# fp32r products that read their moving columns in turn from two halves, in a one-core decoder layer

## The chip, the cores and the metric

The kernel runs on one core of one Trainium2 chip. The metric is the device time of the program in microseconds (us), from its first to its last instruction as the device counts it.

## The reference

One decoder layer over a prompt of 1024 tokens and 8 sample tokens that share the weights, all in float32, with 1024 channels:

```python
h = rmsnorm(x, g_mix);  u = h @ w_in
a, val, gate = u[..., :512], u[..., 512:1024], u[..., 1024:]
glu = val * jax.nn.sigmoid(gate)
ya = pool_mixer(a)                      # trailing means over 2/4/8/16 tokens, a 128x128 map per group
yb = conv_mixer(glu)                    # causal depthwise conv of width 31, LayerNorm, swish
x = x + jnp.concatenate([ya, yb], -1) @ w_out
x = x + cross_attn(rmsnorm(x, g_attn), mk, mv, w_q, w_o)     # 4 heads of 256, 256 memory tokens
h = rmsnorm(x, g_ffn)
x = x + (jax.nn.silu(h @ w_gate) * (h @ w_up)) @ w_down      # 2816 hidden channels
y = rmsnorm(x, g_final)
```

The sample tokens attend to caches of their own (256 tokens each), and the last inputs of the mean pooling and of the convolution are returned as states, as are the memory keys and values.

## The kernel before

Channels lie on the 128 partitions and tokens along the free dimension: T = 1032 columns, first the 512 even prompt tokens, then the 512 odd ones, then the 8 samples. A product takes a 128 x 128 weight tile as the stationary operand and columns of tokens as the moving one, and adds up in PSUM over the channel tiles.

Every operand of a large product is kept as two fp32r parts, a rounded one and the remainder (`split`), and each product is made in three passes, `PASSES = ((0, 0), (0, 1), (1, 0))`: rounded by rounded, rounded weight by remainder, remainder of the weight by rounded. All these products are fp32r. The rest (row sums against `ones_d`, transposes, the pooling map `pmap`) are plain fp32 products.

The widths of the moving operand are few:

- 344 columns (`CW` = T / 3), three spans in three PSUM banks, in `step3` (L497): the projections w_in, w_out, w_q and w_o;
- 512 columns, or 260 columns in two banks (520 in all), in `product` (L1355): the feed-forward part, which forms seven block products for a 2 x 2 block product. A block of 512 tokens takes one bank, a block of 520 (512 tokens and the samples) takes two;
- 256 columns for the keys (L876) and the scores (L1052); 512 for the values (L953) and for probabilities by values (L1110);
- 512 or 260 columns in the last down projection (L1698).

PSUM is read by VectorE (DVE) and ScalarE (ACT). The readers that the change touches are: `gate_out` and `value_out` (from L733), `mixer_in` (L862), `keys` (L880), `values` (L958), `out_a` and `out_b` (L976, L992), `q_group` (L1030, L1031, L1033), the exponentials of the scores (L1069), `pv` (L1114, L1115), `proj_o` (L1221), `plus_sums` (L1371) and `copy_sums` (L1375) with their caller `from_sums`, and `last_down` (L1706). Helpers that lay a view over an operand are `halves` (two halves), `ch3` (three spans) and `as_banks` (the view that matches one or two banks).

The order of the work on each engine comes from a planner in the kernel (`Program.order`), which goes by costs and priorities of the tasks. Those costs depend on widths alone.

The phases on TensorE are, in order: the input projections, keys and values (about 20 to 200 us of the span), the output projection (to about 297), queries, scores and probabilities by values (to 449), w_o (to 540), the gated feed-forward part (about 560 to 980), the down projection (to 1138) and its last part (to 1209).

Of the kernel before, what the change touches and what calls it, by code (L numbers as in the profile page):

```python
# [19 lines left out]
NS = 8  # L20
# [241 lines left out]
def hybrid_step_kernel(ctx: ExitStack, tc: tile.TileContext, io):  # L262
# [34 lines left out]

    def ch3(ap):
        return ap.rearrange("p (c n) -> p c n", c=NCH)

# [190 lines left out]
    def step3(ps, w, wkeys, cols, x, k, first, last, spans=range(NCH), keys=None):  # L491


        def emit(e):
            for p, (wi, xi) in enumerate(PASSES):
                for c in spans:
                    e.matmul(ps[:, c, :CW], w[:, wi, cols], x[:, xi, c * CW : (c + 1) * CW],  # L497
                             start=first and p == 0, stop=last and p == 2)
# [234 lines left out]
    def gate_out(j, ps):  # L733
        t = scr(f"t{j}")
        tk = (t,)
        if j == 0:
            add({"ACT": act(T, True)}, lambda e: e.activation(ch3(t[:]), ps[:, :, :CW], AF.Copy), all3(ps), [tk])
            add({"DVE": dve(T), "Pool": pool_tt(T)}, lambda e: e.tensor_tensor(t[:], t[:], Rx[:], ALU.mult), RX + [tk], [tk], lock=True)
        else:
            add({"DVE": dve(T)}, lambda e: e.tensor_tensor(ch3(t[:]), ps[:, :, :CW], ch3(Rx[:]), ALU.mult), all3(ps) + RX, [tk])  # L740
# [4 lines left out]
    def value_out(j, ps, t):  # L745
# [4 lines left out]
        if j == 0:  # L750
            add({"DVE": dve(T), "ACT": act(T, True)}, lambda e: (
                e.activation(ch3(gb[:, i]), ps[:, :, :CW], AF.Copy) if e is nc.scalar else
                e.tensor_copy(ch3(gb[:, i]), ps[:, :, :CW])), all3(ps), [gk])
            add({"DVE": dve(T), "Pool": pool_tt(T)}, lambda e: e.tensor_tensor(gb[:, i], gb[:, i], t[:], ALU.mult), [gk, (t,)], [gk], lock=True)
        else:
            add({"DVE": dve(T)}, lambda e: e.tensor_tensor(ch3(gb[:, i]), ps[:, :, :CW], ch3(t[:]), ALU.mult), all3(ps) + [(t,)], [gk])
# [102 lines left out]
    def mixer_in(g):  # L859
        ps = group("w_in", xop)  # L860
        ab, ai = a2[g // 2], g % 2
        add({"DVE": dve(T)}, lambda e: e.tensor_tensor(ch3(ab[:, ai]), ps[:, :, :CW], ch3(Rx[:]), ALU.mult), all3(ps) + RX, [(ab, ai)])  # L862
# [6 lines left out]
    def keys(q):  # L869
        ps = mm_buf(f"kps{q}", 1)  # L870
        for i in range(2):
            w, wkeys = w_take("w_k")
            for k in range(KT):
                def emit(e, k=k, i=i, w=w):
                    for p, (wi, xi) in enumerate(PASSES):
                        e.matmul(ps[:, 0, i * NMEM : (i + 1) * NMEM], w[:, wi, block_cols(k)], memg[k // 4][:, xi, k % 4],  # L876
# [4 lines left out]
            kf[:], ps[:, 0].rearrange("p (i m) -> p i m", i=2), Rm().unsqueeze(1).to_broadcast([P, 2, NMEM]), ALU.mult),  # L881
# [62 lines left out]
    def values(c):  # L944
        ps = mm_buf(f"vps{c}", 2)
        for kk in range(4):
            w, wkeys = w_take("w_v")
            for k in (2 * kk, 2 * kk + 1):
                def emit(e, k=k, w=w):
                    col = (k % 2) * 512  # L950
                    for p, (wi, xi) in enumerate(PASSES):
                        for m in range(2):
                            e.matmul(ps[:, m], memg[k // 4][:, xi, k % 4, m * P : (m + 1) * P], w[:, wi, col : col + 512],  # L953
# [3 lines left out]
        for m in range(2):  # L957
            add({"ACT": act(512, True, 1)}, lambda e, m=m: e.activation(  # L958
                vf[:, m], ps[:, m], AF.Copy, scale=rmc[:, 2 * m : 2 * m + 1]), [(ps,), ("rmc",)], [(vf, m)])
# [7 lines left out]
    def out_a(n):  # L967
# [8 lines left out]
        add({"DVE": dve(T)}, lambda e: e.tensor_tensor(ch3(x1[j][:, i]), ps[:, :, :CW], ch3(x1[j][:, i]), ALU.add),  # L976
# [6 lines left out]
    def out_b(n):  # L983
# [8 lines left out]
        add({"DVE": dve(T)}, lambda e: e.tensor_tensor(ch3(x1[j][:, i]), ps[:, :, :CW], ch3(x1[j][:, i]), ALU.add), all3(ps) + [xk], [xk])  # L992
# [35 lines left out]
    def q_group(n):  # L1028
        ps = group("w_q", xq)
        add({"ACT": act(T, True)}, lambda e: e.activation(ch3(qop[n][:, 0]), ps[:, :, :CW], AF.Copy), all3(ps), [(qop[n], 0)])  # L1030
        add({"DVE": dve(T)}, lambda e: e.tensor_tensor(ch3(qop[n][:, 1]), ps[:, :, :CW], ch3(f32(qop[n][:, 0])), ALU.subtract),  # L1031
            all3(ps) + [(qop[n], 0)], [(qop[n], 1)])
        add({"DVE": 0.07}, lambda e: e.tensor_copy(qs[:, n], ps[:, 2, CW - NS : CW]), all3(ps), [("qs", n)])  # L1033

    def scores(n):
# [11 lines left out]
        def emit(e):  # L1047
            for i in range(2):
                tt = 2 * i2 + i
                for dt in range(2):  # L1050
                    for p, (ki, qi) in enumerate(PASSES):
                        e.matmul(bank()[:, i * NMEM : (i + 1) * NMEM], qop[2 * h + dt][:, qi, tt * P : (tt + 1) * P],  # L1052
                                 kk[:, ki, 2 * (h % 2) + dt], start=(dt == 0 and p == 0), stop=(dt == 1 and p == 2))
# [12 lines left out]
        def exps(e):  # L1066
            for i in range(2):
                tt = 2 * i2 + i
                e.activation(pr[:, tt], bank()[:, i * NMEM : (i + 1) * NMEM], AF.Exp, bias=st[:, 2 + i : 3 + i],  # L1069
# [29 lines left out]
    def pv(n):  # L1099
# [4 lines left out]
        for c in range(2):  # L1104
            sl = slice(c * 512, (c + 1) * 512)

            def emit(e, c=c, sl=sl):
                for m in range(2):
                    for p, (vi, pi) in enumerate(PASSES):
                        e.matmul(ps[:, c], v[:, vi, m, col : col + P], pT[h][m][:, pi, sl],  # L1110
# [3 lines left out]
            add({"ACT": act(512, True)}, lambda e, c=c, sl=sl: e.activation(oo[:, 0, sl], ps[:, c], AF.Copy), [(ps, c)], [(oo, 0, c)])  # L1114
# [764 lines left out]
```

## Time and profile before

| | us |
|---|---|
| median of 3 runs | 1219.57 |
| lowest and highest | 1217.78, 1220.19 |
| span of the profiled execution | 1217.6 |
| VectorE busy in the profiled execution | 931.2 |
| ScalarE busy | 524.8 |
| GpSimd busy | 250.1 |

A row of a group has: line, engine, operation, tiles (output, then inputs), shape, count; then busy us of all, mean ns of one; then the idle time of the engine just before them and what ended it. PE is TensorE's products, PEld its weight loads, which run beside the products. Products are pipelined, and the end of each is modelled, so that two neighbours overlap in the rows: what a stream of products costs is read from their starts, or from differences between shapes.

### The profile page before, as it was taken

To read this page: it belongs to the slowest core of one execution; us is meant where nothing else is said; L and a number is where in the kernel's file an instruction comes from. 1 tells how busy PE (TensorE), PEld (TensorE's weight loads), DVE (VectorE), ACT (ScalarE), POOL (GpSimd) and SP (SyncE) were. 2 spreads that over 40 slices of the span, in tenths; PEclk is the share of its full clock that TensorE was granted. 3 is DMA by queue.
4 is the path that set the end of the run, shared out by engine and by line. 5 is a ranking of instruction groups with operands and counts; after the bars stand their busy time and mean duration, and the time that the engine had idled before them with its cause. 6 is when DMAs were issued, how large, how long until landed. Compare 5 with 4: busy or idle time off the path is not lost.

```text
span 1217.6 us, 19433 instructions
## 1 busy us (share of the span) xinstructions
PE 1202.0 (99%) x7736; PEld 1125.9 (92%) x7736; DVE 931.2 (76%) x1548; ACT 524.8 (43%) x718; POOL 250.1 (21%) x297
## 2 busy tenths in 40 slices
PE   9999999999999999999999999999999999999997
PEld 9999988999999979999999999999999999999886
DVE  7899999766258886679877787777867798879754
ACT  7765656455135633454222322233222355544533
POOL 3568842231110102131000000000000024332101
PEclk9999999999999999999999999999999999999998
DMA  7334676326386774421332233222313597678612
GB/s 289 82 77 111 145 213 214 125 105 205 112 263 202 238 272 156 122 87 62 122 113 80 96 114 108 109 80 97 123 70 105 207 310 210 180 185 224 149 51 89
DMA packets 60170, 179.69 MB, mean 148 GB/s; under 512 B 7792, under 2 KB 11568, under 8 KB 58800
## 3 DMA queue, kind: packets, MB, share of 16 engines
q1 hardware_dynamic: 53392, 157.56, 37.1%
q0 software_dynamic: 6256, 20.54, 9.7%
q8 instruction: 60, 0.98, 0.3%
q10 hardware_dynamic: 432, 0.36, 0.1%
q14 instruction: 30, 0.25, 0.1%
HBM read 144.66 MB, written 33.78 MB: 147 GB/s over the span
## 4 chain that ended last, share of the span: by engine, by line
PE 78%; DVE 4%; DMA 1%; issue 1%; ACT 0%; POOL 0%; DVEq 0%; SPq 0%; POOLq 0%; ACTq 0%
PE pr L1355 47%; PE po L497 7%; PE fd L1698 6%; PE ps L497 5%; PE oa L497 4%; PE ob L497 4%; PE sc L1052 1%; DVE spcache_k L1149 1%; PE vps L953 1%; PE pv L1110 1%; DMA sbcache_v<-pd 1%; PE kps L876 0%; PE pmap L896 0%; DMA spcache_k<-in_cache_k 0%; DMA pd<-prow 0%
## 5 line engine op out<-in xcount | busy, mean ns | idle before, releaser
L1355 PEld LDWEIGHTS pr<-ab,wTb 128*128 128x128 f32 x1056 | 131.8, 188 | 3.5
L1355 PE MATMUL pr<-ab,wTa 128*128 128x260 f32 x1056 | 133.6, 282 | 0.2 <-DVE su L1371 0.2
L1355 PE MATMUL pr<-ab,wTb 128*128 128x260 f32 x1056 | 133.0, 282 | 0.0
L1355 PEld LDWEIGHTS pr<-ab,wTa 128*128 128x128 f32 x1056 | 130.8, 188 | 2.4 <-DVE su L1371 0.4
L1355 PE MATMUL pr<-ab,wG 128*128 128x512 f32 x528 | 129.2, 393 | 0.0
L1371 DVE TENSOR_TENSOR su<-pr,su 128x520 f32<-128x520 f32 (+1 forms) x112 | 77.7, 695 | 57.6 <-PE pr L1355 57.4
L1355 PEld LDWEIGHTS pr<-ab,wG 128*128 128x128 f32 x528 | 96.3, 188 | 19.7 <-DVE wG L396 0.4
L497 PE MATMUL ps<-xop,w 128*128 128x344 f32 x720 | 114.1, 320 | 0.0
L497 PEld LDWEIGHTS ps<-xop,w 128*128 128x128 f32 x720 | 113.6, 188 | 0.0
L1355 PEld LDWEIGHTS pr<-hb,dV 128*128 128x128 f32 x768 | 98.8, 188 | 4.1
L1355 PE MATMUL pr<-hb,dV 128*128 128x260 f32 x768 | 100.1, 283 | 0.0
L497 PE MATMUL ps<-xq,w 128*128 128x344 f32 x576 | 94.9, 322 | 0.1
L497 PEld LDWEIGHTS po<-oo,w 128*128 128x128 f32 x576 | 90.8, 188 | 0.6 <-DVE oo L1115 0.4
L497 PE MATMUL po<-oo,w 128*128 128x344 f32 x576 | 91.3, 320 | 0.0
L497 PEld LDWEIGHTS ps<-xq,w 128*128 128x128 f32 x576 | 90.8, 188 | 0.4 <-DMA w<-in_w_q 0.4
L710 DVE SCALAR_TENSOR_TENSOR cacc<-glu,vec,cacc 128x511 f32<-128x511 f32 (+14 forms) x116 | 76.9, 740 | 0.0
L1355 PE MATMUL pr<-hb,dW 128*128 128x512 f32 x288 | 74.5, 394 | 0.1
L385 ACT ACTIVATE w<-raw 128x1024 fp32r<-128x1024 f32 (+1 forms) x37 | 35.0, 950 | 86.7 <-PE po L497 24.4
L1698 PE MATMUL fd<-ho,w 128*128 128x260 f32 (+1 forms) x432 | 69.1, 321 | 0.0
L1698 PEld LDWEIGHTS fd<-ho,w 128*128 128x128 f32 x432 | 62.0, 188 | 6.9 <-issue 0.5
L1382 POOL MEMSET su<- 128x16 f32 x22 | 2.5, 113 | 318.9 <-PE pr L1355 267.7
L1355 PE MATMUL pr<-ab,wU 128*128 128x512 f32 x264 | 64.6, 393 | 0.0
(311 smaller groups left out, 2195.7 us busy)
## 6 DMA issues: line engine op xcount, KB each, us to landing
gr<-in_w_gu SPq DMA_DIRECT2D x44, 512.0 KB, 3.4
hb<-su SPq DMA_DIRECT2D x8, 1040.0 KB, 4.6
hs<-hb SPq DMA_DIRECT2D x16, 520.0 KB, 5.3
dr<-in_w_dn SPq DMA_DIRECT2D x16, 512.0 KB, 4.4
spcache_k<-in_cache_k SPq DMA_DIRECT2D x12, 512.0 KB, 5.7
hs<-hb SPq DMA_DIRECT2D x12, 512.0 KB, 4.6
raw<-in_w_in SPq DMA_DIRECT2D x10, 512.0 KB, 3.3
hb<-he SPq DMA_DIRECT2D x8, 520.0 KB, 2.8
```

Of the source, the lines that this page charges most:

```text
L385: e.activation(dst(0), src(), AF.Copy, scale=1.0 if gain is None else gain)
L497: e.matmul(ps[:, c, :CW], w[:, wi, cols], x[:, xi, c * CW : (c + 1) * CW], start=first and p == 0, stop=last and p == 2)
L710: e.scalar_tensor_tensor(acc[h][:, n:], src[:, : HALF - n], w, acc[h][:, n:], ALU.mult, ALU.add)
L953: e.matmul(ps[:, m], memg[k // 4][:, xi, k % 4, m * P : (m + 1) * P], w[:, wi, col : col + 512], start=(k == 0 and p == 0), stop=(k == KT ...
L1052: e.matmul(bank()[:, i * NMEM : (i + 1) * NMEM], qop[2 * h + dt][:, qi, tt * P : (tt + 1) * P], kk[:, ki, 2 * (h % 2) + dt], start=(dt == ...
L1110: e.matmul(ps[:, c], v[:, vi, m, col : col + P], pT[h][m][:, pi, sl], start=(m == 0 and p == 0), stop=(m == 1 and p == 2))
L1149: e.scalar_tensor_tensor(piece[:, b], piece[:, b], 1.0, bc[:, b], ALU.mult, ALU.mult, accum_out=out(m)[:, first + b : first + b + 1])
L1355: e.matmul(bank(c), w[:, wi, cols(j)], xs[0](j, xi)[:, c * n : (c + 1) * n], start=onto is None and j == 0 and p == 0, stop=j == nj - 1 an ...
L1371: from_sums(sums, "DVE", dve, lambda e, src, sl: e.tensor_tensor(as_banks(o(sl), src), src, as_banks(a(sl), src), op), [akey], [okey])
L1382: add({"Pool": 0.12}, lambda e: e.memset(o(), 0.0), [], keys)
L1698: e.matmul(view(i), w[:, wi, col : col + P], hops[k][:, xi, half, lo - half * HALF + i * width // count : lo - half * HALF + (i + 1) * wid ...
```

## The change

Each fp32r product reads its moving columns in another order. `turns` lays over n columns the view "column 0 of the first half, column 0 of the second half, column 1 of the first half, ...". The output, through `placed`, is written in PSUM in the order in which it comes, so that two neighbouring PSUM columns belong to the two halves. Every reader of such a PSUM tile takes it through `drawn`: the even columns first (the first half), then the odd ones (the second half), against two running halves of its other operands. So the values in SBUF stay where they were. Weights, transposes, row sums and the pooling map are untouched. The instructions, their number and their order on each engine are the same; the planner's costs are too.

```diff
+    def turns(ap):
+        return ap.rearrange("p (h n) -> p n h", h=2)
+
+    def placed(ap):
+        return ap.rearrange("p (n h) -> p n h", h=2)
+
+    def drawn(ap):
+        return ap.rearrange("p (n h) -> p h n" if len(ap.shape) == 2 else "p c (n h) -> p c h n", h=2)
+
+    def drawn3(ps):
+        return drawn(ps[:, :, :CW])
...
+    def ch3h(ap):
+        return ap.rearrange("p (c h n) -> p c h n", c=NCH, h=2)
...
-                    e.matmul(ps[:, c, :CW], w[:, wi, cols], x[:, xi, c * CW : (c + 1) * CW],
+                    e.matmul(placed(ps[:, c, :CW]), w[:, wi, cols], turns(x[:, xi, c * CW : (c + 1) * CW]),
                              start=first and p == 0, stop=last and p == 2)
...
-        add({"ACT": act(T, True)}, lambda e: e.activation(ch3(qop[n][:, 0]), ps[:, :, :CW], AF.Copy), all3(ps), [(qop[n], 0)])
-        add({"DVE": dve(T)}, lambda e: e.tensor_tensor(ch3(qop[n][:, 1]), ps[:, :, :CW], ch3(f32(qop[n][:, 0])), ALU.subtract),
+        add({"ACT": act(T, True)}, lambda e: e.activation(ch3h(qop[n][:, 0]), drawn3(ps), AF.Copy), all3(ps), [(qop[n], 0)])
+        add({"DVE": dve(T)}, lambda e: e.tensor_tensor(ch3h(qop[n][:, 1]), drawn3(ps), ch3h(f32(qop[n][:, 0])), ALU.subtract),
...
     def as_banks(ap, src):

-        return ap if len(src.shape) == 2 else ap.rearrange("p (c n) -> p c n", c=2)
+        return halves(ap) if len(src.shape) == 3 else ap.rearrange("p (c h n) -> p c h n", c=2, h=2)
...
-                        e.matmul(bank(c), w[:, wi, cols(j)], xs[0](j, xi)[:, c * n : (c + 1) * n],
+                        e.matmul(placed(bank(c)), w[:, wi, cols(j)], turns(xs[0](j, xi)[:, c * n : (c + 1) * n]),
                                  start=onto is None and j == 0 and p == 0, stop=j == nj - 1 and p == 2,
                                  skip_group_check=onto is not None)
...
-            add({engine: cost(sl.stop - sl.start)}, lambda e, src=src, sl=sl: emit(e, src(), sl), [key] + r, w)
+            add({engine: cost(sl.stop - sl.start)}, lambda e, src=src, sl=sl: emit(e, drawn(src()), sl), [key] + r, w)
```

The products of the keys, the values, the scores, probabilities by values and the last down projection change in the same way as in `product`, and the readers named above in the same way as in `q_group`.

More of the change, by code (lines that the diff above doesn't have):

```diff
@@ L1051, in emit @@
                     for p, (ki, qi) in enumerate(PASSES):
[L1052 to L1053 removed]
+                        e.matmul(placed(bank()[:, i * NMEM : (i + 1) * NMEM]), qop[2 * h + dt][:, qi, tt * P : (tt + 1) * P],
+                                 turns(kk[:, ki, 2 * (h % 2) + dt]), start=(dt == 0 and p == 0), stop=(dt == 1 and p == 2))
         o = 2 * (h % 2)
@@ L1697, in emit @@
                     for i in range(count):
-                        e.matmul(view(i), w[:, wi, col : col + P], hops[k][:, xi, half, lo - half * HALF + i * width // count : lo - half * HALF + (i + 1) * width // count],
+                        e.matmul(placed(view(i)), w[:, wi, col : col + P],
+                                 turns(hops[k][:, xi, half, lo - half * HALF + i * width // count : lo - half * HALF + (i + 1) * width // count]),
                                  start=(k == 0 and p == 0), stop=(k == 5 and p == 2))
```

39 lines of the change are left out of this document (20 added, 19 removed).

## The prediction

> **What bounds the kernel now.** I read the page first, then the stages, then the single groups of TensorE's work by shape, then the order of time inside one loop. The page says which engine is full:
>
> ```profile
> span 1217.6 us, 19433 instructions
> PE 1202.0 (99%) x7736; PEld 1125.9 (92%) x7736; DVE 931.2 (76%) x1548; ACT 524.8 (43%) x718; POOL 250.1 (21%) x297
> PE 78%; DVE 4%; DMA 1%; issue 1%; ACT 0%; POOL 0%; DVEq 0%; SPq 0%; POOLq 0%; ACTq 0%
> ```
>
> TensorE is busy 99% of the span and carries 78% of the chain that ended last. So the length of one product, times their number, is the time. The table by stage (us, then busy time and count of each engine, the granted clock, DMA share) shows where that holds and which engine stands second:
>
> ```profile
> 20.00:176.00 156.00, 156.00 (x995) 152.63 (x994) 148.84 (x224) 98.03 (x128) 104.98 (x83) 1.00 0.51 129
> 176.00:297.00 121.00, 120.39 (x718) 112.77 (x717) 93.16 (x105) 65.12 (x69) 29.96 (x14) 1.00 0.47 157
> 297.00:449.00 152.00, 148.89 (x963) 140.94 (x961) 99.51 (x339) 62.34 (x126) 16.64 (x24) 1.00 0.65 209
> 449.00:540.00 91.00, 91.00 (x576) 90.79 (x576) 59.85 (x128) 36.00 (x45) 16.35 (x19) 1.00 0.42 143
> 540.00:560.00 20.00, 19.82 (x107) 15.96 (x106) 18.70 (x28) 13.72 (x21) 9.65 (x10) 1.00 0.24 80
> 560.00:1032.00 472.00, 472.00 (x3165) 435.52 (x3165) 368.97 (x514) 151.05 (x195) 24.37 (x55) 1.00 0.37 126
> 1032.00:1138.00 106.00, 105.85 (x703) 97.30 (x702) 90.05 (x131) 49.06 (x57) 32.10 (x38) 1.00 0.74 194
> 1138.00:1209.00 71.00, 70.41 (x441) 62.84 (x440) 35.42 (x60) 34.68 (x58) 8.58 (x11) 1.00 0.32 87
> sum 1197.60, PE 1184.51 PEld 1108.74 DVE 918.32 ACT 510.48 POOL 242.63; mean PE 131.61 PEld 123.19 DVE 102.04 ACT 56.72 POOL 26.96
> ```
>
> The granted clock is 1.00 in every stage, so no throttle stands behind what follows. VectorE is second everywhere, with 149 of 156 us in the first stage and 369 of 472 us in the long one.
>
> Now the length of one product. A busy time that adds modelled ends is no measure of it, so I take differences between shapes. Groups by shape (count, busy us, mean ns of one):
>
> ```profile
> L1355 PE MATMUL pr<-ab,wTa 128*128 128x260 f32 x1056 | 133.6, 282 | 0.2 <-DVE su L1371 0.2
> L1355 PE MATMUL pr<-ab,wG 128*128 128x512 f32 x528 | 129.2, 393 | 0.0
> L532 PE MATMUL Rf_ps<-xss,ones_d 128*128 128x512 f32 x4 | 1.9, 592 | 0.0
> L1729 PE MATMUL fin_ps<-fin,ones_d 128*128 128x260 f32 x4 | 1.2, 382 | 0.0
> ```
>
> The first two are fp32r products, the last two plain fp32 passes, which the change leaves alone. 252 more columns cost an fp32r product 393 − 282 = 111 ns, 0.4405 ns per column. They cost a plain pass 592 − 382 = 210 ns, 0.8333 ns per column. Half of the plain figure is 0.4167. So fp32r takes columns nearly twice as fast as a plain pass, but not quite: 0.0238 ns per column are lost. The starts in one loop of the long stage (start us, busy us) say the same without modelled ends:
>
> ```profile
> 701.37 2.93 PE L1355 MATMUL pr<-ab,wG 128*128 128x512 f32 x12
> 704.14 3.04 PE L1355 MATMUL pr<-ab,wTb 128*128 128x260 f32 x24
> 707.01 3.03 PE L1355 MATMUL pr<-ab,wTa 128*128 128x260 f32 x24
> ```
>
> (704.14 − 701.37) / 12 = 230.8 ns for 512 columns, (707.01 − 704.14) / 24 = 119.6 ns for 260, a slope of 0.441. The Trainium skill, page "TensorE: Matmul & The Clock Gate", section "Back-to-back issue gap", gives about 216 ns for an isolated 512-column product; this trace has 230.8, so here something is in the way.
>
> **The change, part by part.** No instruction is added, dropped or moved on any engine, and no DMA changes. Three things differ. First, 512, 344, 260 or 256 moving columns of a product are read as column 0 of the first half, column 0 of the second half, column 1 of the first, and so on. Second, PSUM is still written in running order, so that side is as before and I cost it at nothing; if that were wrong it would show in the same start-to-start times as the first part. Third, VectorE and ScalarE read every second PSUM column, first the even, then the odd ones, and write running halves.
>
> The reading of moving columns. It can go both ways, and no row shows a moving operand with a step. The loss of 0.0238 ns per column does not come with plain passes, which take a column every 0.8333 ns. Read in turn, each half is asked for a column only every second time, which is that very pace. If the loss comes from asking the same place too fast, the change removes it. If the reader lives on neighbouring columns being fetched together, the change takes that from it, and the nearest row is again the plain pass: a column every 0.8333 ns. So the bounds are 0.4167 and 0.8333 ns per column, from 0.4405 now.
>
> I take the lower bound. The loss is small and steady: the next two rows' starts repeat the 119.6 ns with another weight tile, while VectorE comes and goes.
>
> ```profile
> 709.88 2.94 PE L1355 MATMUL pr<-ab,wG 128*128 128x512 f32 x12
> ```
>
> (709.88 − 707.01) / 24 = 119.6 ns again. A loss as steady as that belongs to the stream itself, not to other engines, and the stream's order is what changes. That is a choice, not a proof: hence the chances below.
>
> What that is worth: 0.0238 × 512 = 12.2 of 230.8 ns, 5.3%; 0.0238 × 260 = 6.2 of 119.6 ns, 5.2%. At 5.25% of PE's busy time the stages could give 8.2, 6.3, 7.8, 4.8, 1.0, 24.8, 5.6 and 3.7 us, together 62. What I let through, stage by stage:
>
> - 20 to 176: VectorE is busy 148.84 of 156, so at most 7 of 8.2 us; I take 5.
> - 176 to 297: some plain passes and LayerNorm waits lie in it; 5 of 6.3.
> - 297 to 449: the chain leaves TensorE for transfers and VectorE here; 4 of 7.8.
>
> ```profile
> 346.55 4.46 DMA pd<-prow
> 351.08 6.49 DMA sbcache_v<-pd
> 360.53 5.54 DVE spcache_k L1149 x32
> 449.07 91.27 PE po L497 x576
> 559.74 472.90 PE pr L1355 x3168
> ```
>
> - 449 to 540: one unbroken run of TensorE in the chain (91.27 us); all 4.8.
> - 540 to 560: a chain through the row factors; 0.
> - 560 to 1032: again one run of 472.90 us; VectorE has 103 us to spare; 24 of 24.8.
> - 1032 to 1138: VectorE at 90 of 106 us, DMA share 0.74; 4 of 5.6.
> - 1138 to 1209: 2.5 of 3.7. Head and tail: 0.
>
> The sum is 49.3 us.
>
> The readers. VectorE reads PSUM as fast as SBUF today:
>
> ```profile
> L1371 DVE TENSOR_TENSOR su<-pr,su 128x520 f32<-128x520 f32 x90 | 62.5, 696 | 41.5 <-PE pr L1355 41.4
> L1379 DVE TENSOR_TENSOR su<-su,Rf 128x520 f32<-128x520 f32 x44 | 30.6, 696 | 5.1 <-ACT su L1407 4.7
> L1375 ACT ACTIVATE su<-pr 128x512 f32<-128x512 f32 x24 | 14.2, 592 | 12.6 <-PE pr L1355 12.0
> ```
>
> 696 ns with an operand in PSUM, 696 ns without: PSUM is not what holds it. With a step of two I take 696 again. A gain is excluded, since the time is already that of an SBUF read, which sets the lower end; as the upper end I take twice, 1392 ns. The cover is VectorE's wait for TensorE, 41.5 us in this one group. ScalarE's readers have more room still (43% busy).
>
> The profiled execution has a span of 1217.6 us against a median of 1219.57 of the runs. 1217.6 − 49.3 = 1168.3 for the span; 1219.57 − 49.3 = 1170.3 for the time.
>
> **The rivals.**
>
> Nothing changes. The reader takes columns at 0.4405 ns whatever their order. For it: two different weight tiles gave 119.6 ns each, as a fixed rate would. Against it: plain passes show no such loss against their own round figure. Time 1219.6, chance 0.13.
>
> The readers become the bound. In the long stage the readers at L1371 are this much:
>
> ```profile
> 560.00:1032.00 472.00, 110.82 (x160) 1.00 0.37 126
> ```
>
> If each takes twice as long, VectorE has 369 + 110.8 = 480 us to do in a stage of 472, and it cannot be full: it now idles 103 us, mostly for TensorE. With half of that left the stage is 531 us. So +8 to +59 us there, and in the first stage, where VectorE is at 95%, some 8 more: 1235 to 1290, I take 1265. It decides from a lengthening of about half (369 + 55 + 51 = 475). For it: no row shows this step. Against it: the equal 696 ns. Chance 0.11.
>
> The columns no longer come together: the slower side. Every column now lies away from the one before. At a plain pass's pace a 512-column product takes 230.8 + 512 × (0.8333 − 0.4405) = 432 ns, 1.87 times; one of 260 takes 222 ns, 1.85 times. With 0.86 of the 1184.5 us on top, less the few plain passes, this adds about 1000 us: 2220. VectorE would then idle most of the time and nothing would hide it. It decides as soon as a column costs more than 0.4405 ns. For it: plain passes prove that 0.8333 is a pace at which this engine does read. Against it: they also compute at that pace, so they don't show what reading could do. The Trainium skill, page "Advanced Engine Details and Errata", section "Memory Cachelines", speaks for this rival: SBUF is read in lines of 16 bytes, full speed needs further accesses to fall on the same line, and at least two hits to a line are needed to hide the access. By that rule each line is hit once at a time here, and the kernel would be near this rival's time; no run here shows it yet, since every moving operand runs on. Chance 0.17. A milder form, in which the loss of 0.0238 grows only some fourfold with more changes of place, adds three times 60 us, about 180: 1400. Chance 0.07.
>
> **How the numbers follow.** Forecast 0.52, nothing changes 0.13, slow readers 0.11, the mild slowing 0.07, the full one 0.17. The time is the forecast's, 1170. Its own range: at the low end all that a product takes over 0.4167 ns per column goes, 17.5 of 230.8 and 11.3 of 119.6 ns, about 8.5%, at the same share let through: 49.3 × 8.5 / 5.25 = 80 us, 1140; at the high end a third of the relief comes, 1203. The range on record must also take in no change, slow readers and the mild slowing: 1140 to 1400, which leaves out the 0.17 of the full slowing. A measurement of this kernel tells about 0.2% (2.4 us) from no change. Faster 0.52, same 0.13, slower 0.11 + 0.07 + 0.17 = 0.35.
>
> **What would show it.** Right: 512-column fp32r products some 12 ns shorter in their mean, 260-column ones some 6 ns, so that their difference falls from 111 towards 105 ns; the readers at L1371's lines still near 696 ns; VectorE's idle time before them shorter; the long stage near 448 us. Wrong: products as long as before (nothing changes); readers clearly over 696 ns with TensorE waiting for VectorE (slow readers); products of 512 columns at 430 ns or more and VectorE half idle (the full slowing). The forecast falls if a product is not shorter, whatever the total does.

## The result, and the profile after

The changed kernel takes 1161.81 us (median of 4 runs, 1160.57 to 1162.97), the kernel before beside it 1219.88 (4 runs, 1217.78 to 1222.16). The ratio is 0.9532, 95% interval 0.9513 to 0.9551: 58 us faster, where the forecast had 49.

First the page's head for the kernel after (span; busy time of each engine; the chain's shares):

```profile
span 1159.6 us, 19434 instructions
...
PE 1125.3 (97%) x7736; PEld 1067.6 (92%) x7736; DVE 926.2 (80%) x1548; ACT 522.6 (45%) x718; POOL 247.6 (21%) x297
...
PE 58%; DVE 12%; DMA 8%; issue 4%; ACT 2%; POOL 1%; SPq 0%; DVEq 0%; POOLq 0%; ACTq 0%
```

TensorE's busy time fell by 1202.0 − 1125.3 = 76.7 us with the same 7736 products. The span fell by 1217.6 − 1159.6 = 58.0. The other 18.7 us are idle time that TensorE did not have before (1217.6 − 1202.0 = 15.6 us then, 34.3 now). So a good three quarters of what the products gave reached the end. VectorE and the transfers, 5% of the chain together before, now hold 20% of it.

The groups by shape of the kernel after (count | busy us, mean ns | idle before and its releasers):

```profile
L1371 PE MATMUL pr<-ab,wTa 128*128 128x260 f32 x1056 | 125.2, 275 | 0.9 <-DVE su L1387 0.9
...
L1371 PE MATMUL pr<-ab,wG 128*128 128x512 f32 x528 | 121.2, 380 | 0.4 <-DVE wG L411 0.4
...
L1387 DVE TENSOR_TENSOR su<-pr,su 128x520 f32<-128x520 f32 x90 | 62.3, 694 | 25.4 <-PE pr L1371 24.2 <-ACT su L1423 0.7
...
L1391 ACT ACTIVATE su<-pr 128x512 f32<-128x512 f32 x24 | 14.1, 586 | 9.4 <-PE pr L1371 9.4
```

The rows of the 512-column product went from 393 to 380 ns, those of 260 columns from 282 to 275, so their difference went from 111 to 105, as written down beforehand. The readers of PSUM are where they were: VectorE 696 then, 694 now; ScalarE 592 then, 586 now. VectorE's idle time before its reader fell from 41.5 to 25.4 us: that is the cover being used up.

Starts in one loop of the long stage (start us, busy us), after:

```profile
909.57 2.75 PE L1371 MATMUL pr<-ab,wG 128*128 128x512 f32 x12
912.16 2.84 PE L1371 MATMUL pr<-ab,wTb 128*128 128x260 f32 x24
914.84 2.84 PE L1371 MATMUL pr<-ab,wTa 128*128 128x260 f32 x24
```

(912.16 − 909.57) / 12 = 215.8 ns for 512 columns, 230.8 before. (914.84 − 912.16) / 24 = 111.7 ns for 260 columns, 119.6 before. By starts the relief is 15.0 and 7.9 ns, a little more than the rows' means say (13 and 7), because the rows carry modelled ends. It is 6.5% and 6.6% of a product. The Trainium skill, page "TensorE: Matmul & The Clock Gate", section "Back-to-back issue gap", gives the gap of an isolated product as N / 2.4 + 2.5 ns, which makes, as an estimate by that page, 215.8 for 512 columns. The kernel after runs at that figure, the kernel before did not.

Stages of the kernel after (start:end, length, busy us and count of PE, PEld, DVE, ACT, POOL, then granted clock, DMA share, GB/s):

```profile
20.00:176.00 156.00, 147.43 (x993) 142.31 (x993) 151.30 (x229) 98.19 (x129) 103.85 (x85) 1.00 0.52 133
...
540.00:910.00 370.00, 370.00 (x2654) 351.06 (x2653) 300.06 (x424) 108.24 (x141) 3.68 (x28) 1.00 0.31 108
910.00:1060.00 150.00, 143.68 (x1012) 134.92 (x1011) 128.23 (x182) 81.33 (x102) 49.69 (x61) 1.00 0.79 233
```

In the first stage TensorE was busy 156.00 of 156 us before; now 147.43, and it got through 993 products, no more than the 995 before, while VectorE (151.30) is nearly full. TensorE's waits in that window add up to the 8.6 us that are missing: the trace puts 7.6 of them on instructions of VectorE (3.2 on the splitting of weights, 2.1 on a reader of the keys) and 1.0 on a transfer. In the gated stage TensorE is still full: 370.00 / 2654 = 139.4 ns a product against 472.00 / 3165 = 149.1. In the down stage 6.3 us of idle time are new.

Where that goes is best read from marks. The view of single tiles gives the first and last start of a group's products. The kernel before:

```profile
L497 PE MATMUL oa<-opa,w x288: 314/319/722, 201.8 to 251.3; 128*128 128x344 f32 x144
...
L497 PE MATMUL po<-oo,w x576: 314/319/427, 449.1 to 540.0; 128*128 128x344 f32 x192
...
L1355 PE MATMUL pr<-ab,wTb x1056: 277/282/289, 553.7 to 978.5; 128*128 128x260 f32 x176
...
L1698 PE MATMUL fd<-ho,w x432: 277/284/686, 1137.9 to 1207.1; 128*128 128x260 f32 x96, 128*128 128x512 f32 x48
```

and the kernel after:

```profile
L512 PE MATMUL oa<-opa,w x288: 309/309/711, 198.4 to 244.6; 128*128 128x344 f32 x144
...
L512 PE MATMUL po<-oo,w x576: 308/309/413, 432.8 to 517.2; 128*128 128x344 f32 x192
...
L1371 PE MATMUL pr<-ab,wTb x1056: 274/275/276, 530.5 to 928.0; 128*128 128x260 f32 x176
...
L1714 PE MATMUL fd<-ho,w x432: 274/275/675, 1084.1 to 1149.2; 128*128 128x260 f32 x96, 128*128 128x512 f32 x48
```

| mark | before | after | ahead by | forecast |
|---|---|---|---|---|
| output projection begins (`oa`, first) | 201.8 | 198.4 | 3.4 | 5 + 5 × 25.8 / 121 = 6.1 |
| w_o begins (`po`, first) | 449.1 | 432.8 | 16.3 | 14 |
| gated part ends (`pr<-ab,wTb`, last) | 978.5 | 928.0 | 50.5 | 18.8 + 24 × 418.5 / 472 = 40.1 |
| last part begins (`fd`, first) | 1137.9 | 1084.1 | 53.8 | 46.8 |
| span | 1217.6 | 1159.6 | 58.0 | 49.3 |

Up to the output projection the gain is small: the input projections end 7.6 us sooner (148.3, now 140.7), and the keys and values behind them, in whose time 5.4 of those 8.6 us of waits lie, lose 4.2 us of that. From w_o's begin to the gated part's end, 529.4 us before, the kernel gained 34.2 us, 6.5%: all that the products gave. Between that mark and the last part it gained 3.3 of 159.4 us, 2%. TensorE's waits in that down stage are now

```profile
PE pr L1371 <- DVE x L1387: 5.2, 5, 1.6
PE pr L1371 <- ACT x L1391: 1.1, 1, 1.1
```

for readers of PSUM (us in total, times, longest). Three things needed runs: why the columns come faster, whether the stepped readers cost anything, and what holds the 18.7 us.

### The profile page after: what moved, and what is told of

Same layout as the page of the kernel before. It is cut to its first block, busy times and chain, and to the rows that moved or that the text cites. A ratio compares the mean times of both kernels' runs of the same rounds, so it can differ in the third digit from the quotient of the medians.

```text
span 1159.6 us, 19434 instructions
## 1 busy us (share of the span) xinstructions
PE 1125.3 (97%) x7736; PEld 1067.6 (92%) x7736; DVE 926.2 (80%) x1548; ACT 522.6 (45%) x718; POOL 247.6 (21%) x297
## 4 chain that ended last, share of the span: by engine, by line
PE 58%; DVE 12%; DMA 8%; issue 4%; ACT 2%; POOL 1%; SPq 0%; DVEq 0%; POOLq 0%; ACTq 0%
PE pr L1371 38%; PE po L512 5%; PE fd L1714 4%; PE ob L512 4%; PE oa L512 3%; DMA dr<-in_w_dn 3%; PE ps L512 2%; DMA xa<-x1d 1%; DVE x L1387 1%; DVE spcache_k L1165 1%; DMA hs<-hb 1%; DVE spcache_v L1165 1%; PE vps L969 1%; DVE hb L411 1%; DVE dV L411 1%
## 5 line engine op out<-in xcount | busy, mean ns | idle before, releaser
L1371 PEld LDWEIGHTS pr<-ab,wTb 128*128 128x128 f32 x1056 | 124.4, 190 | 2.2
L1371 PE MATMUL pr<-ab,wTa 128*128 128x260 f32 x1056 | 125.2, 275 | 0.9 <-DVE su L1387 0.9
L1371 PEld LDWEIGHTS pr<-ab,wTa 128*128 128x128 f32 x1056 | 123.1, 190 | 2.3 <-DVE su L1387 1.1
L1371 PE MATMUL pr<-ab,wTb 128*128 128x260 f32 x1056 | 124.8, 275 | 0.0
L1371 PE MATMUL pr<-ab,wG 128*128 128x512 f32 x528 | 121.2, 380 | 0.4 <-DVE wG L411 0.4
L512 PE MATMUL ps<-xop,w 128*128 128x344 f32 x720 | 106.0, 310 | 2.5 <-DVE w L411 1.5
L512 PEld LDWEIGHTS ps<-xop,w 128*128 128x128 f32 x720 | 105.0, 189 | 3.0 <-DVE w L411 1.7
L512 PE MATMUL ps<-xq,w 128*128 128x344 f32 x576 | 88.0, 311 | 1.0 <-DMA w<-in_w_q 1.0
L512 PEld LDWEIGHTS po<-oo,w 128*128 128x128 f32 x576 | 84.0, 189 | 0.9 <-DVE oo L1131 0.6
L1371 PEld LDWEIGHTS pr<-hb,dW 128*128 128x128 f32 x288 | 50.8, 189 | 11.0 <-DVE x L1387 4.1
```

Of the source, the lines that this page charges most:

```text
L512: e.matmul(placed(ps[:, c, :CW]), w[:, wi, cols], turns(x[:, xi, c * CW : (c + 1) * CW]), start=first and p == 0, stop=last and p == 2)
L1371: e.matmul(placed(bank(c)), w[:, wi, cols(j)], turns(xs[0](j, xi)[:, c * n : (c + 1) * n]), start=onto is None and j == 0 and p == 0, stop ...
```

## The experiments

**Streams by themselves.** A kernel of nothing but streams of 48 equal products, in several orders of the moving columns.

```diff
+    for i in range(48):   # "halves"; the others differ in the two views
+        nc.tensor.matmul(ps[:, :512].rearrange("p (n h) -> p n h", h=2), w[:, i % 8 * P : (i % 8 + 1) * P],
+                         x[:, :512].rearrange("p (h n) -> p n h", h=2), start=i == 0, stop=i == 47)
```

> Not the layer, only streams of 48 products each into one PSUM bank, one order of reading after another; the outputs are zeros. Start to start of one product is asked. Before: 231.2 ns for 512 running fp32r columns; after: 215.6 in turn from two halves. Theory A (neighbouring columns asked from the same small piece of memory collide): every order whose neighbours lie well apart gives about 216: halves, four quarters in turn, every 4th column, every 16th column; every second column lies between; two columns from each half in turn gives about 223 (half of the neighbours still adjoin), four in turn about 227; running gives 231. Theory B (a stall where a running stream goes on to the next piece, hidden only if a second stream is read meanwhile): halves, quarters, twos and fours all give about 216; every 4th and every 16th column, which change the piece at every column with one stream, give 231 or far more. Rival C (the plain pass's pace is what an order without neighbours gets): every 16th column about 430. bfloat16, half the bytes: 216 in both orders under A and B. 128 and 256 columns: after shows 111.6 ns for 256 and for 260 columns alike, so I expect a floor of about 111.6 by the weight load: 128 columns give 111 to 112 in either order, 256 columns 119 running and 111.6 in turn.

The order of time on TensorE (start us, busy us); two neighbouring starts over 48 give one product:

```profile
20.26 11.04 PE L80 MATMUL running<-x,w 128*128 128x512 f32 x48
31.14 10.52 PE L84 MATMUL halves<-x,w 128*128 128x512 f32 x48
41.50 21.92 PE L88 MATMUL evenodd<-x,w 128*128 128x512 f32 x48
63.24 22.32 PE L92 MATMUL fourths<-x,w 128*128 128x512 f32 x48
85.38 20.98 PE L96 MATMUL sixteenths<-x,w 128*128 128x512 f32 x48
106.19 16.18 PE L100 MATMUL twos<-x,w 128*128 128x512 f32 x48
122.20 12.19 PE L104 MATMUL fours<-x,w 128*128 128x512 f32 x48
...
163.64 20.78 PE L116 MATMUL plainout<-xb,wb 128*128 128x512 bf16 x48
184.22 10.56 PE L120 MATMUL bfloat<-xb,wb 128*128 128x512 bf16 x48
194.62 23.41 PE L124 MATMUL bfhalves<-xb,wb 128*128 128x512 bf16 x48
...
223.18 5.52 PE L132 MATMUL smallturn<-x,w 128*128 128x128 f32 x48
228.53 5.97 PE L136 MATMUL narrow<-x,w 128*128 128x256 f32 x48
234.34 5.52 PE L140 MATMUL narrowturn<-x,w 128*128 128x256 f32 x48
```

Running order takes 226.7 ns, in turn from two halves 215.8: 10.9 of the 15.0 ns stand without the rest of the kernel. Every other order is slower than running: every second column 452.9, every fourth 461.3, every sixteenth 433.5, two columns from each half in turn 333.5, four 250.4. A bfloat16 product, fast in running order (216.7), takes some 480 in turn from two halves. Neither of the theories A and B gives this list; the rival's 430 ns came for every sixteenth column, but the halves, whose neighbours lie apart too, are fast. Four quarters in turn take 273.3. Two by-results: writing PSUM with a step of two from a running bfloat16 operand (`plainout`) takes 428.8 ns, twice `bfloat`, so that PSUM has to be written in running order; and 128 or 256 columns in turn take the same time (5.52 us each), 111.7 ns a product, which is what 260 columns take in the kernel: below that the number of columns no longer counts.

**Two readers?** A guess at what separates these orders is how often the even places of a stream (the 1st, 3rd, 5th column read) come to a new 16-byte line, and likewise the odd ones. In running order both kinds walk through every line, two columns each. In turn from two halves each kind has its own half and takes four columns from each line. So the next streams put the two partners of a pair 2, 4 and 8 columns apart, without halves, and stepped through halves.

```diff
+    apart_four:    columns 0 4 1 5 2 6 3 7 | 8 12 9 13 ...
+    apart_two:     columns 0 2 1 3 | 4 6 5 7 ...
+    halves_even:   columns 0 256 2 258 4 260 ...
+    halves_fourth: columns 0 256 4 260 8 264 ...
```

> Streams of 48 products again, outputs zeros. The first streams killed theories A and B: only running (227 ns) and halves (216) were fast in fp32r; every second column 453, every 4th 461, every 16th 433, four quarters 273, two from each half 333, four 250; bfloat16 216 running and 484 in turn from two halves. New theory L (two lanes): an fp32r product takes columns in pairs, the first of each pair and the second of each pair through a reader of its own, and a reader is at full speed when it takes four columns in a row from one 16-byte line, a little short with two, at half speed with one; bfloat16 has one reader, with eight columns to a line. Then, for 512 columns in ns: pairs 4 apart (0,4,1,5,2,6,3,7) 216, pairs 8 apart 216; pairs 2 apart (0,2,1,3) 227; even columns of both halves in turn, then the odd ones (two to a line for each reader) about 227; every 4th column of both halves in turn (one to a line) 430 to 465; bfloat16 running 216, every second column (four to a line) 216, every 4th (two to a line) about 227, every 8th (one to a line) 430 to 490. Rival H (halves are fast because the two places lie far apart, in different parts of the memory): pairs 2, 4 and 8 apart all 227 or slower, even columns of both halves 216. Plain fp32 takes 429 per pass running; under L, if it has one reader at half pace, it loses nothing in turn from halves (429) and nothing by steps.

```profile
21.27 11.04 PE L80 MATMUL running<-x,w 128*128 128x512 f32 x48
32.15 10.52 PE L84 MATMUL halves<-x,w 128*128 128x512 f32 x48
42.51 11.08 PE L88 MATMUL apart_two<-x,w 128*128 128x512 f32 x48
53.43 10.52 PE L92 MATMUL apart_four<-x,w 128*128 128x512 f32 x48
...
74.15 11.08 PE L100 MATMUL halves_even<-x,w 128*128 128x512 f32 x48
85.07 21.91 PE L104 MATMUL halves_fourth<-x,w 128*128 128x512 f32 x48
...
117.20 11.00 PE L112 MATMUL bf_even<-xb,wb 128*128 128x512 bf16 x48
128.04 21.84 PE L116 MATMUL bf_fourth<-xb,wb 128*128 128x512 bf16 x48
149.70 43.38 PE L120 MATMUL bf_eighth<-xb,wb 128*128 128x512 bf16 x48
...
236.55 52.00 PE L128 MATMUL plain_halves<-xin,win 128*128 128x512 f32 x96
```

Distance is not it: partners only 4 columns apart are as fast as halves (10.52 us for 48), and halves with a step of two as slow as running order (11.08). For 512 columns the time goes with the 16-byte lines, counted for the even and for the odd places apart, as if each had a reader of its own that needs about 1.77 ns for a line:

| order | columns read per new line of one reader | measured ns | ns per line |
|---|---|---|---|
| running, apart_two, halves_even | 4 (2 of them its own) | 226.7 to 227.5 | 1.77 to 1.78 |
| evenodd, halves_fourth | 2 (1 its own) | 452.9 | 1.77 |
| fourths, sixteenths | 2 (1 its own) | 461.3, 433.5 | 1.80, 1.69 |
| halves, apart_four | 8 (4 its own) | 215.8 | 3.37: the line is there in time |
| bf_even, bf_fourth, bf_eighth (one reader, 8 columns a line) | 4, 2, 1 | 225.8, 451.3, 900 | 1.76 |
| fours | 4 (2 its own) | 250.4 | 1.96 |
| narrow (256 columns, running) | 4 (2 its own) | 121.0 | 1.89 |

(The last column is the time of one product over its columns, times the second column.) Four columns at full speed take 4 × 0.4215 = 1.686 ns, so at this price running order misses full speed by the 5% between 1.686 and 1.77. The numbers expected for fp32r came; those for bfloat16 did not. With four, two and one column to a line, 216, about 227 and 430 to 490 ns were expected. A price per line, and one reader for all places, gives what was measured. (The granted clock fell to 0.50 within `bf_eighth`, but its products start every 900 ns both before and after that.) For plain fp32, 429 ns a pass was expected in every order: it takes 429 in running order, once its clock is back at 1.00, but 540 in turn from two halves and 450 with a step of two.

The price was drawn from these runs, and it is not the whole of it:

- Every sixteenth column takes 1.69 ns a line, so 1.77 is no fixed cost of a fetch.
- Four columns from each half by turns (`fours`) take 250.4 ns where the price gives 226.7, though no reader comes back to a line there.
- Where readers do come back to a line that they have left (two columns per half by turns, four quarters, bfloat16 and plain fp32 in turn), the times lie between those with the line kept and with it fetched again. How many lines a reader keeps stays open.
- 256 columns in running order take 121.0 ns where 64 lines make 113.3. From 256 to 512 columns the streams add (226.7 − 121.0) / 256 = 0.413 ns a column, which is full speed. Against the same columns in turn, running order loses 10.9 ns with 512 and 9.3 with 256.

The last point leaves a rival: a loss that each product has once, whatever its width, such as one through the weight load that runs beside it. Every product of these streams has a weight load, so no run parts this rival from the price per line. (In the kernel before, the loss did grow with the width: a column between 260 and 512 cost 0.441 ns.) That the order of the columns decides is shown, and so is the part of the 16-byte line and of the even and odd places. Where running order loses its 5% stays open.

The Trainium skill, page "Advanced Engine Details and Errata", section "Memory Cachelines", has lines of 16 bytes in SBUF and asks for at least two hits on a line. The line agrees: a reader that steps over 16 bytes (`evenodd`) is at half speed, and one that steps over 32 (`fourths`) loses next to nothing more. Two hits are not enough by the runs: fp32r in running order, with two hits per reader, is 5% short, and bfloat16 with two (`bf_fourth`) is at half speed.

**The stepped readers alone.** Moving columns and PSUM in running order, readers stepped as in the change.

```diff
     def turns(ap):
-        return ap.rearrange("p (h n) -> p n h", h=2)
+        return ap
     def placed(ap):
-        return ap.rearrange("p (n h) -> p n h", h=2)
+        return ap
```

> Moving columns run on as before, and only the readers take every second PSUM column, so that the tokens of the results stand in another order. Theory (a step of two in PSUM costs VectorE and ScalarE nothing, the gain is all from TensorE's reading): 1219.9 within 0.3%, readers of 520 columns at 692 to 697 ns, products at 231 and 119.7 ns from start to start. Rival (the readers free PSUM sooner, or cost something that the faster products hide): off by more than 5 us.

1217.31 us, ratio 0.9995 (0.9984 to 1.0007): no cost that can be told. Its groups by shape:

```profile
L1387 DVE TENSOR_TENSOR su<-pr,su 128x520 f32<-128x520 f32 x90 | 62.5, 696 | 41.5 <-PE pr L1371 41.3
...
L1371 PE MATMUL pr<-ab,wG 128*128 128x512 f32 x528 | 129.3, 394 | 0.0
```

**One part at a time.** The new order only in `product` and the last down projection (`ff_only`), or everywhere but there (`rest_only`).

```diff
-                    e.matmul(placed(ps[:, c, :CW]), w[:, wi, cols], turns(x[:, xi, c * CW : (c + 1) * CW]),
+                    e.matmul(ps[:, c, :CW], w[:, wi, cols], x[:, xi, c * CW : (c + 1) * CW],
```

> The new order in the feed-forward products and the last down projection alone (lines 1355, 1371, 1375, 1698, 1706 of before), all else as before. By starts there are 1368 products here with 512 columns or so many at 15.5 ns less, and 3168 of 260 columns at 8.1 ns less: 47 us less of TensorE. In the trace of after the span from the end of the row factors to the end wins 28 us in the gated part, 4 in the down projection, 4 at the end. Theory (gains of the parts add up, each after its own waits): 1219.9 - 36 = 1184. Rival (the later part wins only since the earlier one gave DMA and weight preparation a different lead): 1195 or more.

> The complement: the new order in the projections, keys, values, scores and probabilities by values, the feed-forward part as before. TensorE loses 38 us by starts; the trace of after has the row factors done 22 us sooner. Theory (parts add up): 1219.9 - 22 = 1198, and ff_only's gain and this one's come to 58 us together. Rival (what the first part wins is lost again in the later waits): 1210 or more.

Feed-forward part alone: 1182.32 us, ratio 0.971 (0.9688 to 0.9731). The rest alone: 1198.59, ratio 0.9845 (0.9815 to 0.9875). Of the 1217.24 us of the kernel before beside them these are 34.9 and 18.7 us, 53.6 together of the 58: each part pays by itself, and neither needs the other. (The two intervals are some 3 and 4 us wide to either side, so the 4 us that are missing from the sum tell nothing.)

**Another plan for the same products.** The planner's table says 0.0135 + 0.000417 n us for n columns; here it gets the new lengths, with factors of 1.0 for TensorE.

```diff
-    "early": {"PE": (0.93, 0.0), "DVE": (0.93, 0.0), "Pool": (1.0, 0.0), "ACT": (1.0, 0.0)},
+    "early": {"PE": (1.0, 0.0), "DVE": (0.93, 0.0), "Pool": (1.0, 0.0), "ACT": (1.0, 0.0)},
...
-        return (0.0135 + 0.000417 * n) * count
+        return max(0.1117, 0.0023 + 0.000417 * n) * count
```

> The kernel after, with the planner's cost of an fp32r product set to what the trace of after shows (0.0023 us + 0.000417 us per column, at least 0.1117 us) and its factors for TensorE at 1.0; this moves instructions on the other engines, above all in the feed-forward and down parts, where the planner counted 0.122 us for 260 columns. Theory (some of the 19 us by which TensorE's idle time grew comes from an order made for slower products): 1150 to 1158. Rival (the waits are for transfers and VectorE's work, which no order removes): 1159 to 1165.

1165.63 us, ratio 0.957 (0.9554 to 0.9586), no better than the change itself. By the total alone, the order would not be what withholds time. The tiles' marks tell more:

```profile
L512 PE MATMUL po<-oo,w x576: 309/309/413, 444.1 to 529.2; 128*128 128x344 f32 x192
...
L1371 PE MATMUL pr<-ab,wTb x1056: 274/275/378, 542.5 to 940.3; 128*128 128x260 f32 x176
...
L1714 PE MATMUL fd<-ho,w x432: 274/275/675, 1089.1 to 1154.4; 128*128 128x260 f32 x96, 128*128 128x512 f32 x48
```

It comes to w_o 444.1 − 432.8 = 11.3 us later than the kernel after, and then needs only 1089.1 − 940.3 = 148.8 us from the gated part's end to the last part, where the kernel after needs 1084.1 − 928.0 = 156.1. Two plans are mixed up in one number: a worse early one and a better late one.

**A lighter VectorE in the first stage.** 60 of the convolution's steps on VectorE left out (about 44 us), in the kernel before and in the kernel after.

```diff
-        for n in range(16):
+        for n in range(8):
```

> The kernel before with the last 8 of the 16 pairs of convolution taps on VectorE left out in every channel group, 60 instructions of about 735 ns, 44 us of VectorE's work in the first 200 us. TensorE is busy there all the time in before, so little moves: 1210 to 1220.

> The kernel after with the same taps left out. Theory (about half of what TensorE could win up to the output projection, 10 of 21 us, is withheld because VectorE is 97% busy there): with VectorE relieved the gap between this and lighter_before is 65 to 70 us. Rival (it is withheld by transfers or by the first 20 us): the gap stays at 58.

1215.12 us (ratio 0.9984, 0.9975 to 0.9994) and 1154.16 (0.9481, 0.9465 to 0.9497): 61.0 us apart instead of 58. TensorE in the first stage of `lighter_after`:

```profile
20.00:176.00 156.00, 152.04 (x1012) 146.46 (x1011) 145.98 (x219) 107.39 (x140) 81.19 (x68) 0.99 0.52 136
```

152.04 us busy instead of 147.43. So VectorE does stand in the way there. The gap grew by 3 us, not by the 7 to 12 of the theory, and each of the two differences is uncertain by more than 2 us. The run is weaker than it was meant to be, too: the planner gave other work to VectorE, above all some of GpSimd's (busy 247.6 us, now 229.0), so that VectorE's busy time fell by 24 us (926.2 to 901.8) and not by 44, and it is still at 145.98 of 156 us. What a VectorE with time to spare would give back is not shown.

**What lifts 226.7 to 231?** In the kernel before, 512 columns took 230.8 ns, alone 226.7; the order explains only the second.

```diff
+        for k in range(16):
+            nc.vector.tensor_tensor(third[:, 8:520], left[:, :512], right[:, :512], ALU.add)
+        p = stream(name, moving, out)   # likewise beside PSUM reads, ScalarE, GpSimd, transfers
```

> Streams of 48 fp32r products of 512 columns again, nothing of the reference is computed (the outputs are zeros). In the kernel before a 512-column product starts every 231.2 ns, in a stream by itself every 226.7; in the kernel after 215.6, in a stream by itself 215.8. So 4.5 ns of the 15.5 saved are not in the order alone. Here each stream, in running order and in turn from two halves, runs once alone, once with a moving operand that changes from product to product, and once beside each of: VectorE adding in SBUF, VectorE adding from PSUM, ScalarE copying in SBUF, GpSimd adding in SBUF, transfers into SBUF. Theory (SBUF is shared, and a reader that has no time to spare gives way): running order 229 to 234 ns beside VectorE or transfers, in turn 215.8 to 216.5 beside the same. Rival (the change of operand costs it): 231 in running order with changing operands, 226.7 beside any other engine. If neither, all running streams are at 226.7.

```profile
19.30 11.04 PE L89 MATMUL alone<-x,w 128*128 128x512 f32 x48
...
61.81 11.07 PE L89 MATMUL dve<-x,w 128*128 128x512 f32 x48
...
161.65 11.19 PE L89 MATMUL dma<-x,w 128*128 128x512 f32 x48 [1.16 <-POOL w L134]
172.68 10.52 PE L89 MATMUL dma_turn<-x,w 128*128 128x512 f32 x48
```

11.04 us alone, 11.07 beside VectorE, 11.16 beside VectorE reading PSUM, 11.19 beside ScalarE and beside transfers; steady starts stay at 227 ns in each, and at 227 with changing operands. Both theories fell. Narrow products show no such lift: 260 columns took 119.6 ns in the kernel before, 256 alone 121.0. (GpSimd's stream had a granted clock of 0.88 in its stretch and tells nothing.) Several engines at once were not tried, so where the further 4 ns of 512 columns in the kernel come from stays open; that they are gone after the change is plain from its 215.8.

**Half the fetch in the down stage.** The chain of the kernel after goes through the fetch of the down weights.

```diff
-        dma(lambda: dn_raw[u][:], lambda: io["w_dn"][u], 4 * P * D, w=[(dn_raw[u],)])
+        dma(lambda: dn_raw[u][:, :512], lambda: io["w_dn"][u][:, :512], 4 * P * D, w=[(dn_raw[u],)])
```

> The kernel after, but of each weight tile of the down projection's first 16 units only half is fetched (256 instead of 512 KB), and the preparation reads that half twice; the results of the down projection are other numbers, the instructions, their number and sizes on TensorE, VectorE and ScalarE stay. Theory (transfers withhold the gain of that stage: its chain goes through the fetch of these tiles): 1152 to 1157 us, and 61 to 65 us less than the kernel before with the same fetch. Rival (VectorE's preparation withholds it, the transfer is only the last of several): 1160 to 1162, and 57 to 60 less than before with the same fetch.

> The kernel before with the same halved fetch of the down projection's weights. Both theories: 1215 to 1218 us, since TensorE is full there and no transfer is on its chain.

1159.13 us (ratio 0.9523, 0.9499 to 0.9548) and 1216.25 (0.999, 0.998 to 1.0): 57.1 us apart, no more than the 58 with the whole fetch. In its profiled execution TensorE was busy 172.19 of the 175 us from 910, against 168.68 in the kernel after, and from the gated part's end to the last part it took 152.4 us instead of 156.1. So the fetch has some part in those waits. The runs with the halved fetch lie between 1154.82 and 1165.27 us, and their ratio cannot be told from the change's 0.9532: half of the fetch is worth some 4 us in the trace, and nothing that the times can show.

**A better late plan.** TensorE counted at 0.93 of the old table in the gated and the down stage as well, the early plan left as it was.

```diff
-    "gated": {"Pool": (1.02, 0.0), "DVE": (1.0, 0.04), "PE": (0.97, 0.0), "ACT": (1.1, 0.0)},
-    "down": {"DVE": (1.0, 0.083)},
+    "gated": {"Pool": (1.02, 0.0), "DVE": (1.0, 0.04), "PE": (0.93, 0.0), "ACT": (1.1, 0.0)},
+    "down": {"PE": (0.93, 0.0), "DVE": (1.0, 0.083)},
```

> The kernel after, where the planner counts TensorE's work of the gated and the down stage at 0.93 of its table, as it does in the stages ahead; a candidate for a faster kernel. If the order is no lever, 1160 to 1166 us as with the table of measured lengths; if the due times hold transfers back, 1150 to 1157.

1155.09 us (5 runs, 1153.92 to 1157.65), ratio 0.9493 (0.9473 to 0.9512), faster than the kernel before and than the change; against the change's 0.9532 (0.9513 to 0.9551), measured at another time, it is some 5 us, with intervals that just miss each other. Its tiles:

```profile
L512 PE MATMUL po<-oo,w x576: 309/309/413, 432.9 to 517.2; 128*128 128x344 f32 x192
...
L1371 PE MATMUL pr<-ab,wTb x1056: 274/275/378, 530.5 to 927.6; 128*128 128x260 f32 x176
...
L1714 PE MATMUL fd<-ho,w x432: 274/275/675, 1076.6 to 1142.1; 128*128 128x260 f32 x96, 128*128 128x512 f32 x48
```

and its down stage:

```profile
910.00:1060.00 150.00, 149.63 (x1066) 141.46 (x1065) 134.78 (x189) 83.62 (x106) 54.92 (x65) 1.00 0.82 243
```

The early marks are those of the kernel after (432.9, 927.6). The down stage takes 1076.6 − 927.6 = 149.0 us instead of 156.1, with TensorE busy 149.63 of 150 us and the DMA share even higher, 0.82. So the 6.3 us that TensorE waited there come back by another order of the work alone, with the whole fetch; the old order was made for slower products. (The order also sets when each fetch leaves, so this does not clear the fetch as the last link of a wait.) That was the theory that `planned` seemed to have finished; its late half holds.

## Why the prediction was right

- **TensorE bounds the kernel: right.** It is still at 97%, with 58% of the chain.
- **"If the loss comes from asking the same place too fast, the change removes it": right that the order removes it, and narrower than it was put.** The prediction spoke of halves as such. Partners four columns apart do as well, and halves with a step of two don't, so the "place" goes by 16-byte lines. Whether running order loses by asking too fast is not shown: in streams it loses nearly as much with 256 columns (9.3 ns) as with 512 (10.9).
- **The lower bound was in part luck.** The prediction called it a choice, and gave it 0.52. No row that it had told the halves from every second column, which takes 452.9 ns, near the 432 of its slowest rival.
- **"A loss as steady as that belongs to the stream itself": right for most of it.** The stream by itself gives 226.7 − 215.8 = 10.9 of the 15.0 ns; the other 4.1 appear only in the kernel.
- **0.0238 ns per column, "12.2 of 230.8 ns" and 6.2 of 119.6: mis-sized.** By starts 15.0 and 7.9, which is 0.029 and 0.030 ns per column. The difference between two widths, from which 0.0238 came, cannot see a loss that both have alike. The possible gain was 76.7 us of busy time, not 62. W_o and the gated part gave 34.2 us, where it had 4.8 + 21.3 = 26.1: that is 8.1 of the 8.7 us by which the span fell further than forecast. The others cancel nearly: 2.3 more up to w_o, 3.4 less in the down stage, 1.7 more in the last part.
- **What is let through: right as a sum up to w_o** (14 forecast, 16.3 measured), though only 3.4 us had come when the output projection began, and right in the gated stage, where all of it came. **Down stage: forecast too high.** From the gated part's end to the last part it had 46.8 − 40.1 = 6.7 us, and 3.3 came. The allowance named VectorE's load and the DMA share of 0.74; the runs show that another order of the work gives the waits back with both as high as before. Of the 18.7 us of new idle time 6.3 lie there and 8.6 in the first stage, where the lighter VectorE brought back 4.6 (147.43 to 152.04). That VectorE held most of the rest there is what the trace's waits say; no run has tried it further.
- **The readers stay at 696 ns: right,** 694, and by themselves free (ratio 0.9995).
- **Writing PSUM in running order costs nothing: right** and worth the care, since a step of two in the write takes 428.8 ns.
- **The rivals.** Nothing changes: out, by 230.8 to 215.8. Slow readers: out. Columns no longer together: out for this order, but true of its neighbours; every second column takes 452.9 ns, and two columns by turns from each half take 333.5. The 16-byte line that it rests on does count; in this order, as the streams read, even and odd places still find four columns each in a line. The mild slowing: out for this order as well; four quarters in turn, at 273.3 ns, come near it.

## What to carry to other kernels

An fp32r product that runs through its moving columns one by one was 5 to 7% slower here than one whose even and odd places stay in 16-byte lines of their own. Pairs taken from two halves, with PSUM written in running order and read with a step of two, get that back at no cost that these runs could tell; pairs four or eight columns apart are as fast in streams, and were not tried in the kernel. Neighbouring orders cost up to twice the time, and bfloat16 wants running order, so measure the order in a stream of products by itself first. When the bounding engine gets faster, give its new speed to the planner stage by stage: one number for all stages hid a gain in one behind a loss in another.

## What the runs showed of the hardware that was not expected

- The moving operand of an fp32r product of 512 columns behaves, in most orders, as if even and odd places had a reader each, at some 1.77 ns per 16-byte line; bfloat16 as if one reader served all (225.8, 451.3 and 900 ns with four, two and one column to a line).
- fp32r products of 128, 256 and 260 columns all take 111.7 ns in turn, so here widths below some 265 columns (111.7 / 0.4215, an estimate) save nothing.
- A bfloat16 product of 512 columns that writes PSUM with a step of two takes 428.8 ns instead of 216.7; VectorE and ScalarE read PSUM with a step of two at no cost (694 and 586 ns for 520 and 512 columns).
- VectorE, ScalarE or transfers (286 GB/s in that stretch), each alone beside a stream of products in running order, left its steady 227 ns as they were.
